# A fused two-layer kernel: when the steps of a second triangular inverse are issued, where a recurrence state is copied, and when a block of it is loaded

## The chip, the cores and the metric

The kernel runs on one core of a Trainium2 chip. Its time is the device time of one execution in microseconds, as the chip's profiler or the timed runs give it. The core has five instruction queues: TensorE (matmuls, PE in the profile, with the weight loads listed as PEld), VectorE (DVE), ScalarE (ACT), GpSimd (POOL) and SyncE (SP). Each takes its instructions in the order in which they were issued to it. Matmuls write to PSUM, which VectorE and ScalarE read.

## What is computed

Layer one is an RWKV-7 mixer over 256 tokens with 32 heads of 64, layer two an attention layer with compressed, selected and windowed keys; each is added to the residual, and a norm ends it. What matters here is the recurrence of the first layer:

```python
def wkv7_scan(r, w, k, v, a, b):
    ...
    def step(S, inp):
        r_t, w_t, k_t, v_t, a_t, b_t = inp
        sa = jnp.einsum('bhvk,bhk->bhv', S, a_t)
        S = S * w_t[:, :, None, :] + sa[..., None] * b_t[:, :, None, :] + v_t[..., None] * k_t[:, :, None, :]
        return S, jnp.einsum('bhvk,bhk->bhv', S, r_t)
    S0 = jnp.zeros((B, H, N, N), jnp.float32)
    _, o = lax.scan(step, S0, seq)
    return jnp.moveaxis(o, 0, 1)
```

After it each head's output is normalized, a bonus is added, it is multiplied by a gate, and it goes through the output projection w_o.

## The kernel before

Every large product is made of fp32 numbers split into a high and a low part, in three matmuls. ScalarE writes the high part of a weight tile (line 206, whi), VectorE the low part (line 191, wlo).

The recurrence is done in chunks: the 256 tokens are four chunks of 64. In a chunk the step-by-step recurrence becomes a triangular system of 64 by 64 for each head, whose inverse is needed. Two heads are an index x, and four heads (two of x by two of h) make a unit U; there are eight units. The inverse of a 64 by 64 triangle is put together from its two diagonal 32 by 32 triangles and a product of matrices. stage_t (line 799) computes all the 32 by 32 inverses on VectorE, for sixteen heads at a time, one triangle on each of the 128 partitions: stage_t(0) serves units 0 to 3 and ends before the scan, stage_t(1) serves units 4 to 7 and runs beside units 0 to 2 of it. It doubles the size of the inverted blocks four times, to 2, 4 (lines 834 to 848), 8 and 16 (dot, line 849: a multiplication on line 854, a sum on line 857, in up to two halves). Then it stores the inverse (tnd), ScalarE transposes it by four copies (line 882), and it is stored once more (yvd).

The scan loop (line 1261) goes over the units, and for each over twelve visits v: chunk c = v // 3 and part p = v % 3 of phase (line 1074).
- p = 0: TensorE removes the old state's part (line 1072, with the masked products AMA, "ama" in the trace) and adds that of the state (line 1088); ScalarE copies the result to X (line 1090).
- p = 1: TensorE multiplies X by the inverse Yb (line 1095); ScalarE copies to uv (line 1097).
- p = 2: TensorE makes the output (line 1101) and the state's increment pS (line 1104). VectorE makes the new state nxt: a copy for the first chunk (line 1107), an addition afterwards (line 1109). ScalarE scales it to the decayed state sP for the next chunk (line 1114). Then VectorE takes the output's statistics (line 1123, sta).

Between these parts the loop issues the work of the neighbours. NORM says in which visit the output of the unit before is normalized ("nmr", "v", "b", "g", "+", "z" on VectorE, pairs of digits on ScalarE, lines 1143 to 1157). AUX says in which visit the next unit is prepared: B0 and B1 (transposes, line 1041), G and Y (lines 1022 and 1031: the lower left block of the inverse, from Yb and A10), A0 and A1 (products, lines 1055 and 1057), M2, M0, M1 (masks on VectorE, line 1063: ama and amr), T (the finished unit's transposes, line 1164). scale_r (line 1005) makes VectorE's ar and mb (lines 1010 and 1011). load_y (line 908) loads Yb on GpSimd's queue in two parts of four transfers, q = 1 and q = 0; G needs the part q = 1. fill(n) puts n filler steps of the dense projections on TensorE (lines 626 to 628), as many as FILLL and FILL say for each visit; they keep TensorE at work while the small chain goes over the other engines.

The order of all five queues in this stage is the order of the program text: it is written by hand (manual_schedule, line 973). Only the inverse is placed by a planner, Sched (line 97). It holds a clock t in nanoseconds that fillers and phases move on. pump() goes once through the background generators: one that is due issues its instructions up to its next yield; a yielded number is the wait until it is due again, a yielded function is a condition that must hold first. In the scan stage_t(1) is the only one. Its waits are a cost estimate times PACE (line 821); at 0 each pump takes one step. The prologue of the scan (PROLOGUE, lines 1243 to 1258) pumps as often as its "V" step says; unit 0 does so nine times more at visit 2 (line 1281). load_a(4), in visit 8 of unit 2, requires that the second inverse has been issued (line 898), and pumps until it is.

```python
        for v in range(12):
            phase(U, v // 3, v % 3)
            ...
            sch.pump()
            if v == 11:
                finish(U, "rg")
```

finish(U, "rg") (line 1127) takes the statistics of a unit on VectorE, then a power on GpSimd (line 1136) and a copy "bon" out of PSUM on ScalarE (line 1137).

Of the kernel before, what the change touches and what calls it, by code (L numbers as in the profile page):

```python
# [12 lines left out]
AF = mybir.ActivationFunctionType  # L13
# [56 lines left out]
KPO = 3  # L70
KLAG = 2
AUX = {2: ("B0",), 3: ("G",), 4: ("B1", "Y"), 7: ("A0",), 9: ("A1",), 10: ("T", "M2"), 11: ("M0", "M1")}
NORM = {1: ("nmr", "v", "02"), 2: ("b", "24"), 5: ("46",), 6: ("68",), 7: ("g",), 8: ("+", "z")}
FILLL = (3, 4, 4, 0, 0, 5, 4, 0, 4, 0, 4, 4)
PROLOGUE = ("R0", "R1", 6, "G", "B0", 4, "I", "Y", "B1", 2, "A0", 2, "V10", "A1", "M2", "M0", "M1", 2)
ZHOOK = 9
PACES, PACE = (0.0, 1.8, 1.8, 1.8), [0.0]
FILL = (3, 4, 4, 0, 0, 5, 4, 0, 4, 0, 4, 4)
FILLO, LASTFILL = 4, 36
QZ = (0, 25, 24, 1, 2, 23, 22, 21, 3, 20, 19, 18, 4, 17, 16, 15, 14, 13, 12, 11, 10)  # L80
# [137 lines left out]
def hybrid_kernel(ctx: ExitStack, tc: tile.TileContext, a: dict, out: bass.AP):  # L218
    nc = tc.nc
    V, S, G, PE = nc.vector, nc.scalar, nc.gpsimd, nc.tensor  # L220
# [578 lines left out]
    def stage_t(b):  # L799
# [49 lines left out]
        def dot(out, aa, bb, ni, nj, kk):  # L849
            x = X[:, :ni * nj * kk].rearrange("p (i j k) -> p i j k", i=ni, j=nj)  # L850
            m = 2 if b and ni * nj * kk > 512 else 1
            for i0, i1 in [(ni * n // m, ni * (n + 1) // m) for n in range(m)]:
                sh = [128, i1 - i0, nj, kk]
                V.tensor_tensor(x[:, i0:i1], aa[:, i0:i1, None, :].to_broadcast(sh), bb[:, None, :, :].to_broadcast(sh), op=OP.mult)  # L854
                if b:
                    yield pace(1.1 * (i1 - i0) * nj * kk)
                V.tensor_reduce(out[:, i0:i1], x[:, i0:i1], axis=AX.X, op=OP.add)
                yield pace(1.2 * (i1 - i0) * nj * kk) if b else pace(2.3 * ni * nj * kk + 60.0)

# [31 lines left out]
    NU = NK // 2  # L891
# [182 lines left out]
    def phase(U, c, p):  # L1074
# [18 lines left out]
        elif p == 1:  # L1093
            for x, h in each:
                PE.matmul(pu[R[1 - h], 1 - x], Yb[U % 2][H(x, h), x, c, :], XS[U][H(x, h), x, :], start=False, **mm)
            for h in range(2):
                S.activation(uv[R[1 - h], :, c, h, :], pu[R[1 - h]], AF.Copy)
            sch.t += 200
        else:
            for x, h in each:  # L1100
                PE.matmul(O[H(x, h), x], AMR[U % 2][:, h, x, c, :], uv[:, 1 - x, c, h, :], start=False, **mm)
            if c < NCH - 1:
                for x, h in each:
                    PE.matmul(pS[R[h], x], BKT[U % 2][x][:, c, h, :], uv[:, 1 - x, c, h, :], start=False, **mm)
                nxt = scan.tile([128, 2, 64], F32, name="S", bufs=3)
                if c == 0:
                    V.tensor_copy(nxt, pS)
                else:
                    V.tensor_tensor(nxt, SST[U][1], pS, op=OP.add)
                dec = None  # L1110
                if c < NCH - 2:
                    dec = scan.tile([128, 2, 64], F32, name="sP", bufs=2)
                    for x in range(2):
                        S.activation(dec[:, x], nxt[:, x], AF.Copy, scale=PCH[U][:, x, c:c + 1])
                SST[U] = (nxt, dec)
            sch.t += 700

# [143 lines left out]
    for U in range(NU):  # L1261
        PBK[U] = pair_tile(U % 2)
        P = U - 1
        PACE[0] = PACES[min(U + 1, 3)]
        for v in range(12):
            phase(U, v // 3, v % 3)
            if v % 3 == 2:
                stats(U, v // 3)
            sch.pump()
            if v == 11:  # L1270
                finish(U, "rg")
                if U + 2 < NU:
                    load_y(U + 2, qs=(1,))
            if v == 0:
                if U and U + 1 < NU:
                    load_y(U + 1, qs=(0,))
# [32 lines left out]
    U = NU - 1  # L1309
# [520 lines left out]
```

## Time and profile before

| | us |
|---|---|
| median of three timed runs | 1134.08 |
| the three runs | 1135.6, 1134.08, 1131.72 |
| the profiled execution | 1132.65 |
| its span, first to last instruction | 1130.9 |
| scan loop, first matmul of unit 0 to the end of unit 7 | about 366 to 566 |

A profile line such as "365.98 0.40 PE L1072 MATMUL pair<-uv,ama ... x8 [1.65 <-DVE ama L1063]" reads: at 365.98 us, for 0.40 us, eight matmuls of line 1072 on TensorE that write a tile of name pair from uv and ama; TensorE had been idle for 1.65 us, and what ended that was VectorE's instruction of line 1063 that writes ama. A line of the waits gives the waiting engine, the line and the releaser, then the sum in us, the number of times and the longest. A line of the stretches gives the window and its length, then for PE, PEld, DVE, ACT and POOL the busy us and the number of instructions, then the granted TensorE clock (1.00 is full speed), the busy share of the DMA engines and GB/s. A line of the instruction groups gives the number of instructions, their busy us and the mean ns of one. A line on a source line's instructions gives their least, middle and longest ns, and the first and last start. "who waited for it" lines give us and times.

### The profile page before, as it was taken

How to read it: one execution, taken by the hardware profiler on the slowest of the kernel's cores; microseconds unless marked ns; L12 is line 12 of the kernel's file. 1: busy time of each engine (PE TensorE's matmuls, PEld its weight loads, DVE VectorE, ACT ScalarE, POOL GpSimd, SP SyncE). 2: the span in 40 equal slices, each digit the busy share in tenths (PEclk: the TensorE clock that was granted, in tenths of full speed). 3: DMA queues.
4: the chain of work that ended last, by engine and by line, in shares of the span. 5: the costliest groups of instructions: out<-in, count | busy, mean ns of one | idle time of the engine just before them, and what ended most of it. 6: DMA issues, size and time to landing. Idle time of an engine off the chain costs nothing.

```text
span 1130.9 us, 25651 instructions
## 1 busy us (share of the span) xinstructions
PE 1105.1 (98%) x9496; PEld 979.3 (87%) x9496; DVE 829.2 (73%) x1776; ACT 723.8 (64%) x1704; POOL 316.1 (28%) x412
## 2 busy tenths in 40 slices
PE   8999999999999998999999999999999999999997
PEld 7788899898988988898888888888989999999887
DVE  6999876689897887566667876764666877766564
ACT  7667877577764446565556766665656777766553
POOL 1300045424347446453000010100323332332012
PEclk9999999999999989999999999999999999999999
DMA  7558878877879868775578658585746365544862
GB/s 256 156 193 258 231 209 261 241 215 219 258 216 285 211 170 217 205 191 147 159 233 272 211 175 286 179 276 165 195 145 165 100 155 140 136 131 149 299 196 103
DMA packets 234462, 226.33 MB, mean 200 GB/s; under 512 B 50608, under 2 KB 184096, under 8 KB 233952
## 3 DMA queue, kind: packets, MB, share of 16 engines
q1 hardware_dynamic: 228976, 219.14, 65.5%
q0 software_dynamic: 4896, 4.95, 1.9%
q8 instruction: 75, 1.23, 0.5%
q10 hardware_dynamic: 464, 0.59, 0.1%
q14 instruction: 51, 0.42, 0.1%
HBM read 200.48 MB, written 24.15 MB: 199 GB/s over the span
## 4 chain that ended last, share of the span: by engine, by line
PE 80%; DVE 9%; DMA 3%; issue 3%; ACT 3%; SPq 1%; POOL 1%; POOLq 0%; DVEq 0%; ACTq 0%
PE bank L609 13%; PE bank L611 13%; PE bank L608 13%; PE bank L626 7%; PE bank L628 7%; PE bank L627 7%; PE bank L234 5%; DVE wlo L191 3%; PE pair L611 1%; PE pair L608 1%; PE pair L609 1%; DMA Yb<-yvd 1%; PE bank L1181 1%; ACT whi L206 1%; DVE invX L854 1%
## 5 line engine op out<-in xcount | busy, mean ns | idle before, releaser
L191 DVE TENSOR_TENSOR wlo<-wraw,whi 128x512 fp32r<-128x512 f32 (+2 forms) x616 | 438.7, 725 | 160.2 <-ACT whi L206 156.3
L206 ACT ACTIVATE whi<-wraw 128x512 fp32r<-128x512 f32 (+2 forms) x664 | 403.4, 618 | 188.2 <-PE bank L611 69.3
L626 PE MATMUL bank<-mh,whi 128*128 128x256 f32 (+1 forms) x800 | 236.5, 296 | 0.4 <-ACT whi L206 0.4
L628 PE MATMUL bank<-mh,wlo 128*128 128x256 f32 (+1 forms) x800 | 229.6, 287 | 0.4 <-issue 0.4
L627 PE MATMUL bank<-ml,whi 128*128 128x256 f32 (+1 forms) x800 | 229.2, 286 | 0.0
L609 PE MATMUL bank<-wlo,mh 128*128 128x512 f32 (+3 forms) x576 | 218.0, 379 | 0.8 <-DVE wlo L191 0.7
L611 PE MATMUL bank<-whi,ml 128*128 128x512 f32 (+3 forms) x576 | 215.3, 376 | 0.0
L608 PE MATMUL bank<-whi,mh 128*128 128x512 f32 (+3 forms) x576 | 190.3, 377 | 0.6 <-ACT Vt L1474 0.3
L626 PEld LDWEIGHTS bank<-mh,whi 128*128 128x128 f32 (+1 forms) x800 | 153.0, 191 | 5.9 <-ACT whi L206 1.0
L628 PEld LDWEIGHTS bank<-mh,wlo 128*128 128x128 f32 (+1 forms) x800 | 153.0, 191 | 2.1 <-issue 0.6
L627 PEld LDWEIGHTS bank<-ml,whi 128*128 128x128 f32 (+1 forms) x800 | 153.4, 192 | 1.5
L609 PEld LDWEIGHTS bank<-wlo,mh 128*128 128x128 f32 x576 | 108.3, 188 | 17.9 <-DVE wlo L191 1.8
L611 PEld LDWEIGHTS bank<-whi,ml 128*128 128x128 f32 x576 | 108.3, 188 | 16.2
L608 PEld LDWEIGHTS bank<-whi,mh 128*128 128x128 f32 x576 | 107.0, 188 | 17.1 <-ACT Vt L1474 0.7
L191 POOL TENSOR_TENSOR wlo<-wraw,whi 128x512 fp32r<-128x512 f32 (+2 forms) x48 | 57.5, 1198 | 186.1 <-ACT whi L206 162.9
L609 PE MATMUL bank<-wlo,kvh 128*128 128x512 f32 x192 | 76.0, 396 | 0.0
L611 PE MATMUL bank<-whi,kvl 128*128 128x512 f32 x192 | 75.2, 392 | 0.0
L608 PE MATMUL bank<-whi,kvh 128*128 128x512 f32 x192 | 66.5, 391 | 0.0
L422 ACT ACTIVATE mh<-mtmp 128x256 fp32r<-128x256 f32 x95 | 37.7, 410 | 17.7 <-DVE mtmp L429 16.6
L429 DVE SCALAR_TENSOR_TENSOR mtmp<-xx,prm,xn 128x256 f32<-128x256 f32 x95 | 46.7, 503 | 0.1
L609 PEld LDWEIGHTS bank<-wlo,kvh 128*128 128x128 f32 x192 | 36.1, 188 | 7.8 <-issue 0.4
L423 DVE TENSOR_TENSOR ml<-mtmp,mh 128x256 fp32r<-128x256 f32 x95 | 40.2, 438 | 2.6 <-ACT mh L422 2.5
(350 smaller groups left out, 1908.9 us busy)
## 6 DMA issues: line engine op xcount, KB each, us to landing
wraw<-in_a_w_rkvz_dram SPq DMA_DIRECT2D x128, 512.0 KB, 5.2
wraw<-in_kv_w_dram SPq DMA_DIRECT2D x48, 512.0 KB, 4.6
wraw<-in_b_w_in_dram SPq DMA_DIRECT2D x40, 512.0 KB, 4.2
wraw<-in_a_w_o_dram SPq DMA_DIRECT2D x32, 512.0 KB, 4.6
wraw<-in_b_w_o_dram SPq DMA_DIRECT2D x32, 512.0 KB, 3.8
spd<-sp SPq DMA_DIRECT2D x16, 642.0 KB, 5.5
spl<-spd SPq DMA_DIRECT2D x16, 642.0 KB, 6.5
wraw<-in_b_w_in_dram SPq DMA_DIRECT2D x24, 384.0 KB, 3.2
```

Source lines behind the costliest of these rows:

```text
L191: eng.tensor_tensor(lv, src, hv.bitcast(F32), op=OP.subtract)
L206: self.nc.scalar.activation(hv, src, AF.Copy)
L234: return fn(*args, **kw)
L422: S.activation(h, src, AF.Copy)
L423: V.tensor_tensor(l, src, h.bitcast(F32), op=OP.subtract)
L429: V.scalar_tensor_tensor(m, xx[:, k, :], mu[:, k:k + 1], xn[:, k, 1:], op0=OP.mult, op1=OP.add)
L608: PE.matmul(o, mh[:, ts], wh[:, 0, :], start=k == ends[0], stop=False)
L609: PE.matmul(o, mh[:, ts], wl[:, 0, :], start=False, stop=False)
L611: PE.matmul(o, ml[:, ts], wh[:, 0, :], start=False, stop=k == ends[1])
L626: PE.matmul(o, wh[:, s, :], mh, start=k == 0 and first, stop=False, **kw)
L627: PE.matmul(o, wh[:, s, :], ml, start=False, stop=False, **kw)
L628: PE.matmul(o, wl[:, s, :], mh, start=False, stop=k == NK - 1, **kw)
```

## The change

Four edits, all in the scan stage.
1. The inverse's multiplications and sums (lines 854 and 857) are not issued in visits 0, 1, 2 and 11 of units 1 to 7: a flag HOLD is set there, and the generator yields a condition that it be cleared. To make up for it PACE is 0.9 instead of 1.8 from unit 1 on. The prologue pumps five times ("V5") instead of ten ("V10").
2. The normalization's step "b" (line 1147) moves from visit 2 to visit 4.
3. The first chunk's state is copied out of PSUM by ScalarE instead of VectorE, and ScalarE makes the decayed state of that chunk straight from PSUM instead of from the copy.
4. The part q = 1 of Yb for the unit after the next is loaded in visit 10, instead of visit 11 behind finish(U, "rg").

```diff
-NORM = {1: ("nmr", "v", "02"), 2: ("b", "24"), 5: ("46",), 6: ("68",), 7: ("g",), 8: ("+", "z")}
+NORM = {1: ("nmr", "v", "02"), 2: ("24",), 4: ("b",), 5: ("46",), 6: ("68",), 7: ("g",), 8: ("+", "z")}
...
-PROLOGUE = ("R0", "R1", 6, "G", "B0", 4, "I", "Y", "B1", 2, "A0", 2, "V10", "A1", "M2", "M0", "M1", 2)
+PROLOGUE = ("R0", "R1", 6, "G", "B0", 4, "I", "Y", "B1", 2, "A0", 2, "V5", "A1", "M2", "M0", "M1", 2)
...
-PACES, PACE = (0.0, 1.8, 1.8, 1.8), [0.0]
+PACES, PACE, HOLD = (0.0, 1.8, 0.9, 0.9), [0.0], [False]
...
                 sh = [128, i1 - i0, nj, kk]
+                if HOLD[0]:
+                    yield lambda: not HOLD[0]
                 V.tensor_tensor(x[:, i0:i1], aa[:, i0:i1, None, :].to_broadcast(sh), bb[:, None, :, :].to_broadcast(sh), op=OP.mult)
                 if b:
                     yield pace(1.1 * (i1 - i0) * nj * kk)
+                if HOLD[0]:
+                    yield lambda: not HOLD[0]
                 V.tensor_reduce(out[:, i0:i1], x[:, i0:i1], axis=AX.X, op=OP.add)
...
                 if c == 0:
-                    V.tensor_copy(nxt, pS)
+                    S.activation(nxt, pS, AF.Copy)
                 else:
                     V.tensor_tensor(nxt, SST[U][1], pS, op=OP.add)
...
-                        S.activation(dec[:, x], nxt[:, x], AF.Copy, scale=PCH[U][:, x, c:c + 1])
+                        S.activation(dec[:, x], (nxt if c else pS)[:, x], AF.Copy, scale=PCH[U][:, x, c:c + 1])
...
         for v in range(12):
+            HOLD[0] = U > 0 and v in (0, 1, 2, 11)
             phase(U, v // 3, v % 3)
             if v % 3 == 2:
                 stats(U, v // 3)
             sch.pump()
+            if v == 10 and U + 2 < NU:
+                load_y(U + 2, qs=(1,))
             if v == 11:
                 finish(U, "rg")
-                if U + 2 < NU:
-                    load_y(U + 2, qs=(1,))
```

## The prediction

> **What bounds the kernel now.** I read the page first, then the waits between 365 and 545 us (the stage in which the diff acts), then the same stage stretch by stretch, and last the order of single instructions on VectorE, GpSimd and TensorE.
>
> ```profile
> span 1130.9 us, 25651 instructions
> PE 1105.1 (98%) x9496; PEld 979.3 (87%) x9496; DVE 829.2 (73%) x1776; ACT 723.8 (64%) x1704; POOL 316.1 (28%) x412
> ...
> PE 80%; DVE 9%; DMA 3%; issue 3%; ACT 3%; SPq 1%; POOL 1%; POOLq 0%; DVEq 0%; ACTq 0%
> ```
>
> TensorE is busy 98% of the span and makes 80% of the chain that ended last. So a microsecond that TensorE stands still, or runs at half clock, is a microsecond of the end; work on another engine costs nothing until TensorE waits for it. In the scan stage it waits for these:
>
> ```profile
> PE pair L1022 <- DMA Yb<-yvd: 2.2, 6, 0.9
> PE pair L1072 <- DVE sta L1123: 2.1, 2, 1.2
> PE pair L1095 <- ACT X L1090: 1.7, 2, 0.9
> PE pair L1072 <- DVE ama L1063: 1.6, 1, 1.6
> PE bank L1041 <- DVE mb L1011: 1.3, 1, 1.3
> ```
>
> These five kinds of wait are 8.9 us. The stage loses more than that, because a wait also delays what hangs behind it and because the clock falls (the figure after the five engines' busy times, the granted clock):
>
> ```profile
> 365.00:390.00 25.00, 24.02 (x456) 22.00 (x456) 20.54 (x67) 10.02 (x29) 9.68 (x18) 0.86 0.93 239
> 390.00:415.00 25.00, 23.08 (x472) 20.91 (x471) 20.48 (x47) 12.52 (x38) 12.83 (x21) 0.86 0.68 170
> ...
> 451.02:469.48 18.46, 17.42 (x401) 15.65 (x400) 10.11 (x23) 10.32 (x31) 7.86 (x15) 1.00 0.75 198
> ```
>
> In the first two rows the clock is 0.86 and VectorE is busy 20.5 of 25 us; in the third it is 1.00 and VectorE has 10.1 of 18.5. The difference on VectorE is the second inverse, which is spread over units 0 to 2. To get the whole loss I compare equal stretches: every unit does the same twelve visits, and the first matmuls of visits 0, 3, 6 and 9 (line 1072) mark them.
>
> ```profile
> 365.98 0.40 PE L1072 MATMUL pair<-uv,ama 64*64 64x64 f32 x8 [1.65 <-DVE ama L1063]
> ...
> 375.24 0.34 PE L1072 MATMUL pair<-uv,ama 64*64 64x64 f32 x8
> ...
> 390.92 0.34 PE L1072 MATMUL pair<-uv,ama 64*64 64x64 f32 x8
> ...
> 407.26 0.34 PE L1072 MATMUL pair<-uv,ama 64*64 64x64 f32 x8
> ...
> 418.47 0.34 PE L1072 MATMUL pair<-uv,ama 64*64 64x64 f32 x8
> ...
> 440.16 0.34 PE L1072 MATMUL pair<-uv,ama 64*64 64x64 f32 x8
> ...
> 452.19 0.34 PE L1072 MATMUL pair<-uv,ama 64*64 64x64 f32 x8
> ...
> 458.17 0.34 PE L1072 MATMUL pair<-uv,ama 64*64 64x64 f32 x8
> ...
> 476.42 0.34 PE L1072 MATMUL pair<-uv,ama 64*64 64x64 f32 x8
> ...
> 483.16 0.34 PE L1072 MATMUL pair<-uv,ama 64*64 64x64 f32 x8
> ...
> 494.66 0.34 PE L1072 MATMUL pair<-uv,ama 64*64 64x64 f32 x8
> ...
> 501.04 0.34 PE L1072 MATMUL pair<-uv,ama 64*64 64x64 f32 x8
> ...
> 506.02 0.34 PE L1072 MATMUL pair<-uv,ama 64*64 64x64 f32 x8
> ...
> 511.59 0.34 PE L1072 MATMUL pair<-uv,ama 64*64 64x64 f32 x8
> ...
> 524.74 0.34 PE L1072 MATMUL pair<-uv,ama 64*64 64x64 f32 x8
> ...
> 530.63 0.34 PE L1072 MATMUL pair<-uv,ama 64*64 64x64 f32 x8
> ```
>
> Unit 5 is the clean one. Its visits 0-2 take 501.04 - 494.66 = 6.38 us, visits 3-5 take 506.02 - 501.04 = 4.98, visits 6-8 take 511.59 - 506.02 = 5.57. Against it:
> - before unit 0: the wait of 1.65 us for the masked products ama;
> - unit 0, visits 0-2: 375.24 - 365.98 = 9.26, which is 2.88 too long with no wait in it: the first stretch at half clock;
> - unit 1, visits 0-5: 407.26 - 390.92 = 16.34 against 11.36, 4.98 too long: waits for sta and X, and the second stretch at half clock (the like of the first, about 2.9);
> - unit 2, visits 0-8: 440.16 - 418.47 = 21.69 against 16.93, 4.76 too long: waits for mb, sta, X and the transposed inverse's copies on ScalarE;
> - visits 3-5 of units 3, 4 and 6, where Yb arrives late: 5.98, 6.74 and 5.89 against 4.98, 3.67 too long in all.
>
> The sum is 1.65 + 2.88 + 4.98 + 4.76 + 3.67 = 17.94 us. This is all that the change can take away.
>
> **The prologue, "V10" to "V5".** Ten pumped steps of the inverse stand on VectorE ahead of ama, for which TensorE waits. In the trace nine instructions start from the first row below up to the second; five pumped steps fewer are just these nine.
>
> ```profile
> 363.15 0.22 DVE L837 TENSOR_TENSOR invX<-invA,invT 128x64 f32<-128x64 f32 x1
> ...
> 365.24 0.68 DVE L1063 TENSOR_TENSOR ama<-bank,cst 128x512 f32<-128x512 f32 x1
> ```
>
> So ama moves up by 365.24 - 363.15 = 2.09 us, more than the wait of 1.65; its products come ahead of the last filler matmuls, so nothing else holds it. The wait goes to 0, and TensorE itself is late next. The nine instructions move into visits 0 and 1 of unit 0, where VectorE waited for TensorE; they cost nothing there unless B0 (line 1041) or sta become late, by at most their own 2.09 us. I take 0.
>
> **The inverse out of visits 11, 0, 1 and 2, at twice the pace.** I worked the scheduler's clock through both versions. Now the long steps (128x512 and 128x384) lie also in visits 11 to 2 of units 1 and 2, ahead of the mask, of mb, of the state copy and of sta. Afterwards none does, except one multiplication in visit 11 of unit 0, which is not held. Seventeen steps then fall into visits 3 to 10 of unit 1 (seven of 128x512, six of 128x384, four of 128x256), and the last six into visits 3 to 5 of unit 2. The inverse is still placed before load_a(4) in visit 8 of unit 2, which asks for it; only the four copies on ScalarE (line 882) and the store slip from visits 4-6 to visits 7-8. Their mean times:
>
> ```profile
> L857 DVE TENSOR_REDUCE invM<-invX 128x32 f32<-128x512 f32 x2 | 1.4, 683 | 0.0
> ...
> L854 DVE TENSOR_TENSOR invX<-invA,invM 128x384 f32<-128x384 f32 x2 | 1.7, 872 | 0.0
> ...
> L857 DVE TENSOR_REDUCE invM<-invX 128x32 f32<-128x384 f32 x2 | 1.1, 542 | 0.0
> ...
> L857 DVE TENSOR_REDUCE invM<-invX 128x64 f32<-128x256 f32 x1 | 0.4, 422 | 0.0
> ```
>
> Seventeen steps are 7 x 0.683 + 6 x 0.542 + 4 x 0.422 = 9.7 us. The like stretch of unit 3, from sta of visit 2 to sta of visit 11, is the row 451.02:469.48: 10.1 us of VectorE in 18.5 us, and 17.5 without unit 3's 1.0 us for Yb. So VectorE needs 9.7 + 10.1 = 19.8 us where TensorE needs 17.5. Where TensorE itself still loses the 0.7 us that I leave it in that stretch (below), it is 1.6; so VectorE comes out of unit 1 between 1.6 and 2.3 us late, and the first matmuls of unit 2 wait that long for sta of visit 11. I take 1.9, the middle. That is a new wait which this trace does not have. Of the other waits 0.7 is left at visits 3-4 of unit 1 (half of the two there, since vt and wlo still stand before sta), and 0.9 in unit 2, where the six last steps and ScalarE's four copies lie. "b" at visit 4 takes one 128x512 step out of the way of the state; it is in the sum of unit 1, since that row holds it.
>
> **State on ScalarE.**
>
> ```profile
> L1107 DVE COPY S<-pair x8: 275/291/292, 373.5 to 546.9; 128x128 f32<-128x128 f32 x8
> ...
> L1114 ACT ACTIVATE sP<-S,pc x32: 332/340/351, 373.9 to 553.7; 128x64 f32<-128x64 f32 x32
> ...
>   ACT bon L1137: 14.6, 8
> ...
> 499.53 0.35 DVE L1123 BATCH_NORM_STATS2 sta<-pair 128x6 f32<-128x64 f32 x2
> ```
>
> Eight copies of 0.29 us leave VectorE, where each stood behind vt and wlo, and the two scalings wait for TensorE alone. ScalarE gets eight copies; no row shows one, so I bound it by the first two rows, 0.29 and 0.34 us, and hide it behind the filler matmuls of visit 2. The change adds a wait. The third row (of those who waited for sta, line 1123) shows that a read of a unit's PSUM tile on ScalarE, bon, waits for VectorE's read of the same tile, 8 times of 8. So sta of visit 2 will wait for the copy and both scalings, 0.29 + 2 x 0.34 = 0.97 us; behind it on VectorE stands a wlo, and line 1072 of visit 3 waits for sta. In unit 5 sta ended at 499.88, 1.16 us ahead of that matmul at 501.04: so 0 in units 3 to 7, and 0.97 each, 7.8 in all, if that cover were gone. A scaling out of PSUM instead of SBUF I bound by -0.05 and +0.05 us, the difference of those two rows, and take 0.
>
> **The half clock.** Both stretches (2.88 and about 2.9 us) begin at waits, of 1.65 us for ama and of 1.2 for sta with one for X (under 0.9) close behind. I take them for their consequence, and gone with them. [...]
>
> **Yb one visit earlier.**
>
> ```profile
> 470.56 1.66 POOL L1136 TENSOR_TENSOR rg<-rg,half 128x8 f32<-128x8 f32 x1 [6.55 <-DVE rg L1135]
> 472.18 1.15 POOL L914 DMA_DIRECT2D Yb<-yvd  x2
> ```
>
> The first part of Yb is issued on GpSimd's queue behind rg, which waited 6.55 us for VectorE. Issued in visit 10 it is past both, needs only that visit's line 1095 and load_a's eight issues before it, and leads by rg's 1.66 us at least, against waits of at most 0.9. All 3.67 go. Rg can be held back by four issues of about 0.57, less than its 6.55. In unit 2 the inverse's store slips, but load_a asks for it first.
>
> **The sum.** 17.94 less 1.9, 0.7 and 0.9 is 14.4 us. The profiled execution took 1132.65 us (its span of 1130.9 and 1.75 around it), so its like takes 1118.2. The three timed runs have a mean of 1133.8, 1.1 above the profiled one: I forecast 1119.3. No edit of the stage after the scan is made; I cost it at nothing.
>
> **Rivals.**
>
> *Half clock behind the new wait.* A wait of 1.65 and the pair for sta and X were each followed by half clock; the 1.3 for mb was not. The new wait of 1.9 at the start of unit 2 lies above that. If it brings one stretch, 2.9 comes back: 1122.2. Against it: the visits around it are filled with large matmuls.
>
> *The half clock has another cause.* If the two stretches don't come from the waits, they stay, 2.88 + 2.9: 1125.1. For it: nothing but their order in time ties them. Against it: unit 3, with waits of under 1 us, runs at 1.00 (third row of the stretches). [...]
>
> *VectorE is later than I think.* The row of 0.872 us for 128x384 shows what a step can take beside GpSimd, 0.33 more than the other. If all seventeen take that, 5.6 us more come on top of the 1.9: 1124.9, and 1127.8 with a half-clock stretch.
>
> *The waits only move.* VectorE does the same work but for eight copies. If units 0 to 2 lose as much in other places, only Yb's part is won, 3.67 at most: 1130.1 to 1134.
>
> *Slower: the state on ScalarE in every unit.*
>
> ```profile
> L206 ACT ACTIVATE whi<-wraw 128x512 fp32r<-128x512 f32 (+2 forms) x664 | 403.4, 618 | 188.2 <-PE bank L611 69.3
> ```
>
> There the copy stands behind two scalings like sP and a whi of 0.62, 1.30 us. With the 0.97 of the copy and its scalings sta is 2.27 us later than the state's matmuls allow; 1.16 is covered. Seven units would lose 1.1 each, 7.8, which still leaves it faster. From a gap of about 1.65 us, where half clock set in, each would lose 2.9 more: 7 x (1.1 + 2.9) = 28 us, thus 1147.3. For it: ScalarE's queue is fixed by hand. Against it: it waits for VectorE now, and would start sooner.
>
> **How the numbers follow.** Forecast 0.46, half clock behind the new wait 0.20, another cause 0.10, VectorE later 0.10, moved waits 0.08, slower 0.06. A measurement of this kernel tells 0.3%, 3.4 us, from no change. So faster has 0.86, same 0.08, slower 0.06. The forecast's own range is 1117.4 (a new wait of 1.6 and nothing else left) to 1121 (2.3, and 0.2 a unit for sta); the timed runs scatter by 2 us below their mean, so 1115 is the low end; the high end of 1127 takes in the half clock, its other cause and VectorE's lateness up to near its end. That leaves out 0.18.
>
> **What would show it.** Right: no wait for ama before unit 0; clock 1.00 in both stretches; 6.4 us for visits 0-2 of units 1 and 2; no wait of line 1022 for Yb; sta waiting for sP on VectorE; a wait of 1 to 2.3 us for sta at the first matmul of unit 2. Wrong: a VectorE without idle time through all of unit 1 and waits over 3 us behind it; clock below 1 in the scan; line 1072 waiting for sta in visit 3 of units 3 to 7.

## The result and the profile after

The changed kernel took 1128.18 us, the median of five runs (1126.91 to 1129.11), beside 1133.96 for the kernel before: a ratio of 0.9938, 95% interval 0.9921 to 0.9956. That is 5.8 us less, where the forecast said 14.4, and above the top of its range (1127). Six later runs of the same kernel had a median of 1125.89 beside 1134.68 (0.9919, 0.9894 to 0.9944), 8.8 us less: inside the range, but still far from 14.4. The direction was right; the size was not.

The page of the changed kernel, with the span, the engines' busy times and the chain that ended last:

```profile
span 1126.6 us, 25651 instructions
PE 1100.2 (98%) x9496; PEld 973.9 (86%) x9496; DVE 830.0 (74%) x1768; ACT 723.0 (64%) x1712; POOL 316.1 (28%) x412
...
PE 79%; DVE 10%; DMA 4%; issue 3%; ACT 3%; POOL 1%; SPq 0%; POOLq 0%; DVEq 0%; ACTq 0%
```

Eight instructions went from VectorE to ScalarE; nothing else changed in kind. TensorE's waits between 365 and 545 us in it:

```profile
PE pair L1076 <- DVE sta L1127: 2.9, 5, 1.0
PE bank L626 <- ACT whi L206: 1.6, 1, 1.6
PE pair L1092 <- issue: 1.3, 1, 1.3
PE pair L1059 <- issue: 1.1, 1, 1.1
PE pair L1099 <- ACT X L1094: 0.7, 1, 0.7
```

(In the changed kernel the lines from 854 on stand two, and those from 857 on four further down: 1022 is 1026, 1072 is 1076, 1088 is 1092, 1095 is 1099, 1123 is 1127.) The waits for ama, mb and Yb are gone. sta has more than before (2.9 for 2.1), and so have the waits named "issue", in which TensorE waited for nothing that the profile shows; the kernel before has 2.3 us of them in the scan with its prologue. The clock in the two stretches that were at 0.86:

```profile
365.00:390.00 25.00, 24.01 (x513) 21.64 (x513) 21.89 (x78) 10.55 (x30) 13.28 (x24) 1.00 1.10 280
390.00:415.00 25.00, 23.66 (x501) 21.51 (x500) 23.56 (x54) 13.81 (x41) 13.50 (x24) 1.00 0.78 194
```

It is 1.00 in this execution. VectorE, in the third busy figure, is busy 23.6 of 25 us in unit 1. The marks (first matmul of a group of three visits) of units 2 and 5:

```profile
415.47 0.34 PE L1076 MATMUL pair<-uv,ama 64*64 64x64 f32 x8
424.24 0.34 PE L1076 MATMUL pair<-uv,ama 64*64 64x64 f32 x8 [0.71 <-DVE sta L1127]
429.37 0.34 PE L1076 MATMUL pair<-uv,ama 64*64 64x64 f32 x8
436.51 0.34 PE L1076 MATMUL pair<-uv,ama 64*64 64x64 f32 x8
...
489.99 0.34 PE L1076 MATMUL pair<-uv,ama 64*64 64x64 f32 x8
496.50 0.34 PE L1076 MATMUL pair<-uv,ama 64*64 64x64 f32 x8
501.62 0.34 PE L1076 MATMUL pair<-uv,ama 64*64 64x64 f32 x8
```

Unit 2 still takes 436.51 - 415.47 = 21.04 us for visits 0-8 (21.69 before). Unit 5, which nothing was to touch, is longer: 6.51 for 6.38 in visits 0-2, 5.12 for 4.98 in visits 3-5.

One profile is a small sample of a kernel whose runs scatter by 2 us, so I took two of the kernel before and three of the changed one. The table adds their stretches, each a difference of two marks, from the first matmul of line 1022 in the scan's prologue to visit 9 of unit 7.

| stretch | before (us) | after (us) | change of the means | forecast |
|---|---|---|---|---|
| prologue to unit 0 | 10.82, 10.97 | 9.98, 8.76, 8.27 | -1.9 | -1.65 |
| unit 0, visits 0-2 | 9.26, 7.81 | 7.23, 7.45, 7.49 | -1.15 | -2.88 |
| unit 0, visits 3-11 | 15.68, 16.10 | 16.33, 17.08, 16.52 | +0.75 | 0 |
| unit 1, visits 0-5 | 16.34, 13.57 | 12.52, 13.64, 13.37 | -1.8 | -4.28 |
| unit 1, visits 6-11 | 11.21, 11.22 | 11.89, 11.21, 11.22 | +0.2 | +1.9 |
| unit 2, visits 0-8 | 21.69, 23.42 | 21.04, 22.57, 20.39 | -1.2 | -3.86 |
| units 3, 4, 6, visits 3-5 | 18.61, 18.38 | 15.37, 15.35, 17.99 | -2.3 | -3.67 |
| units 3 to 6, visits 0-2 | 25.50, 25.50 | 26.46, 26.96, 27.56 | +1.5 | 0 |
| unit 3, visits 6-8 | 6.23, 6.44 | 7.26, 7.11, 5.87 | +0.4 | 0 |
| the rest | | | -0.2 | 0 |
| all | 206.10, 204.25 | 198.90, 200.51, 199.34 | -5.6 | -14.4 |

(The forecast's new wait of 1.9 us stands ahead of the first matmul of unit 2, so it falls into the last visits of unit 1.) The sum agrees with the timed 5.8. No row is worse than forecast by more than 2.7 us: the shortfall is spread.

### The profile page after: what moved, and what is told of

Read it like the earlier page. It is cut to its first block, busy times and chain, and to the rows that moved or that the text cites. A ratio compares the mean times of both kernels' runs of the same rounds, so it can differ in the third digit from the quotient of the medians.

```text
span 1126.6 us, 25651 instructions
## 1 busy us (share of the span) xinstructions
PE 1100.2 (98%) x9496; PEld 973.9 (86%) x9496; DVE 830.0 (74%) x1768; ACT 723.0 (64%) x1712; POOL 316.1 (28%) x412
## 4 chain that ended last, share of the span: by engine, by line
PE 79%; DVE 10%; DMA 4%; issue 3%; ACT 3%; POOL 1%; SPq 0%; POOLq 0%; DVEq 0%; ACTq 0%
PE bank L609 13%; PE bank L611 13%; PE bank L608 13%; PE bank L626 7%; PE bank L628 6%; PE bank L627 6%; PE bank L234 5%; DVE wlo L191 4%; ACT whi L206 1%; PE pair L611 1%; PE pair L608 1%; PE pair L609 1%; DVE invX L856 1%; PE bank L1185 1%; DMA vt<-vd 1%
```

## The experiments

The theory after the first look at the trace was that every edit wins what it aims at, but that the copy on ScalarE, the loads ahead of rg and VectorE's lateness give part of it back. The rivals: the waits only move; the half clock has another cause; the loss is chance. All medians below come with the kernel before on the same chip (1133.87, 1134.85, 1133.94, 1134.25 and 1134.68 us in the five groups).

### The edits one by one

Yb alone, on the kernel before:

```diff
+            if v == 10 and U + 2 < NU:
+                load_y(U + 2, qs=(1,))
             if v == 11:
                 finish(U, "rg")
-                if U + 2 < NU:
-                    load_y(U + 2, qs=(1,))
```

> The kernel before with only the Yb loads moved (two DMAs of the q = 1 half issued ahead of rg). Theory A (the gains of the three edits exist one by one, and the trace of the changed kernel shows them: Yb -3.2, half clock and the wait for ama -6.6, the state copy on ScalarE +0.26 a unit, the rest new waits): 3.2 us faster than before, line 1022 no longer waits for Yb in visits 3 to 5 of units 3, 4 and 6, rg on GpSimd runs about 2 us later behind the DMA issues without a TensorE wait from it, since the copy of the state does not stand behind O on ScalarE here. Rival B (waits only move): under 1 us faster, with a wait for sta at line 1072 in place of the one for Yb.

Measured 1129.91 us, ratio 0.997 (0.9958 to 0.9983), 4.0 less; no wait for Yb was left. But a wait of 0.34 to 0.41 us for X at line 1095 took the place of part of it: visits 3 to 5 of units 3 to 6 take 5.37 to 5.42, not 4.98.

The inverse's edits alone (V5, pace, HOLD, "b"):

```diff
-PACES, PACE = (0.0, 1.8, 1.8, 1.8), [0.0]
+PACES, PACE, HOLD = (0.0, 1.8, 0.9, 0.9), [0.0], [False]
...
+            HOLD[0] = U > 0 and v in (0, 1, 2, 11)
```

> The kernel before with only the edits of the inverse's steps (V5, pace, held visits, the b step to visit 4). Theory A: granted clock 1.00 in units 0 and 1 (two stretches of about 2.9 us back) and no wait for ama ahead of unit 0, less about 1 us of VectorE's lateness at the start of unit 2: 4.5 to 6 us faster than before. Rival B (the half clock has another cause than the gaps of the first units): a granted clock below 1 stays in units 0 and 1, and the gain is under 1.5 us. [...]

Measured 1129.46, ratio 0.9967 (0.9953 to 0.9981), 4.4 less. No wait for ama was left, and visits 0-2 of unit 1 took 6.38 as forecast; but visits 0-2 of unit 2 took 7.99, and a stretch at half clock stood in its visits 3 to 5. Two stretches around it:

```profile
413.00:424.00 11.00, 8.41 (x164) 7.32 (x164) 10.67 (x27) 5.38 (x16) 7.15 (x11) 0.99 0.63 145
424.00:431.00 7.00, 7.00 (x95) 6.15 (x91) 3.36 (x8) 3.97 (x11) 0.39 (x1) 0.52 0.70 220
```

TensorE was busy 8.41 of 11 us, and for the next 7 the clock was 0.52. This is near the place of the prediction's first rival, but not that rival: no wait for sta stands there, and the last waits ahead of the stretch are 1.07 and 0.20 us for Yb, at 422.60 and 423.08, which the early load takes away.

The state on ScalarE alone:

```diff
-                    V.tensor_copy(nxt, pS)
+                    S.activation(nxt, pS, AF.Copy)
...
-                        S.activation(dec[:, x], nxt[:, x], AF.Copy, scale=PCH[U][:, x, c:c + 1])
+                        S.activation(dec[:, x], (nxt if c else pS)[:, x], AF.Copy, scale=PCH[U][:, x, c:c + 1])
```

> The kernel before with only the copy of the first chunk's state on ScalarE and sP straight from PSUM. Theory A: the chain by which the first matmul of visit 3 waits is longer by 0.26 us in each unit, and more where the copy stands behind O on ScalarE: 2 to 3 us slower than before, visits 0 to 2 of unit 5 up from 6.38 to 6.5. Rival B (the prediction: nobody waits for the copy, as the chain through sP and sta sets the time): within 1 us of before, visits 0 to 2 of unit 5 at 6.38.

Measured 1133.31, ratio 0.9991 (0.9975 to 1.0006): no difference that can be told. Visits 0 to 2 of units 3 to 6 stay at 6.37 and 6.38, as the prediction had it. So theory A missed here: by itself the copy costs the chain nothing in these units.

The changed kernel without the state's edit:

> The changed kernel with the copy of the state back on VectorE, and sP made from the copy. Theory A: the 0.26 us of each unit come back (2.1), and the waits for sta in visit 3 of units 2 and 3, where the copy stood behind O in ScalarE's queue, shrink by another 1: 2 to 3 us faster than the changed kernel, 1125 to 1126. Rival B: VectorE, which is nearly full in unit 1, is later still with the copy, and the time is the changed kernel's or up to 1 us more.

Measured 1127.13, ratio 0.9942 (0.9925 to 0.9958): the changed kernel's time, where theory A had 1125 to 1126. Visits 0-2 of unit 1 fell from 7.41 to 6.62 us and those of units 4 to 6 to 6.37 and 6.38, but visits 3-5 rose to 5.37 and more. In these two pairs (with and without it, on the kernel before and on the changed one) the state's edit is worth nothing that can be told. In the second it only shifts where a delay on ScalarE shows.

### Where that delay comes from

The same instruction in unit 4 of the kernel before, and then of the changed kernel, both on VectorE:

```profile
473.36 0.15 DVE L1143 SCALAR_TENSOR_TENSOR nmr<-mv,rg 128x8 f32<-128x8 f32 x1
```

```profile
470.45 0.76 DVE L1147 SCALAR_TENSOR_TENSOR nmr<-mv,rg 128x8 f32<-128x8 f32 x1
```

In units 4 to 6 nmr takes 0.15 to 0.16 us in each kernel that loads the part q = 1 of Yb in visit 11, and 0.76 to 0.77 in each that loads it in visit 10, and O on ScalarE waits for it. What follows stands in ScalarE's queue; here is the run without the state's edit, on ScalarE and then on TensorE:

```profile
469.90 0.68 ACT L1161 ACTIVATE O<-pair,nmr,rg 128x64 f32<-128x64 f32 x2
470.48 0.48 ACT L1046 ACTIVATE bkt<-bank 128x384 f32<-128x384 f32 x1
470.85 0.63 ACT L206 ACTIVATE whi<-wraw 128x512 fp32r<-128x512 f32 x1
471.37 0.27 ACT L1094 ACTIVATE X<-pair 128x128 f32<-128x128 f32 x1
...
471.70 0.34 PE L1099 MATMUL pair<-X,Yb 64*64 64x64 f32 x8 [0.36 <-ACT X L1094]
```

ScalarE runs without a pause from O to X, and TensorE waits 0.36 us for X. With the state on ScalarE the same lateness hits the copy and, through sP and sta, the first matmul of visit 3. Unit 2 of the changed kernel shows it at its worst, ScalarE and then VectorE:

```profile
421.90 0.70 ACT L1161 ACTIVATE O<-pair,nmr,rg 128x64 f32<-128x64 f32 x2 [2.67 <-DVE nmr L1147]
422.50 0.63 ACT L206 ACTIVATE whi<-wraw 128x512 fp32r<-128x512 f32 x1
423.02 0.27 ACT L1111 ACTIVATE S<-pair 128x128 f32<-128x128 f32 x1
423.18 0.53 ACT L1118 ACTIVATE sP<-pair,pc 128x64 f32<-128x64 f32 x2
...
423.74 0.36 DVE L1127 BATCH_NORM_STATS2 sta<-pair 128x6 f32<-128x64 f32 x2 [0.72 <-ACT sP L1118]
```

O waits 2.67 us for nmr, the copy waits behind O and whi, sta waits 0.72 for sP, and the matmul at 424.24 (above) waits 0.71 for sta. The edit took the copy off VectorE and put it behind VectorE.

I first took nmr's 0.6 us for the four q = 0 loads that GpSimd issues beside it, and moved those to visit 2, once with the state on VectorE and once as in the change:

```diff
-                if U and U + 1 < NU:
-                    load_y(U + 1, qs=(0,))
...
+            if v == 2 and U and U + 1 < NU:
+                load_y(U + 1, qs=(0,))
```

> The changed kernel with the copy of the state on VectorE (as in the run without the state's edit, 1127.1) and the four Yb loads of the q = 0 half issued on GpSimd in visit 2, behind nmr and pc and ars, instead of in visit 0. Theory A (nmr takes 0.76 us instead of 0.16 where GpSimd issues those four loads beside it, ScalarE's O and with it the X of visit 3 start that much later, and TensorE waits at line 1099): nmr back at 0.16 in units 2 to 6, the waits for X at line 1099 (3.5 us in 6 places) down by 1.5 to 2 us, 1125 to 1125.6. Rival B (the 0.76 us have another cause): nmr stays at 0.76, and the time is within 1 us of 1127.1.

> The changed kernel, the copy of the state on ScalarE as there, with the four Yb loads of the q = 0 half issued in visit 2 as in the run beside this one. Theory A: nmr at 0.16 us, O on ScalarE 0.6 us earlier, and the copy of the state, which is queued behind O, with it: visits 0 to 2 of units 4 to 6 from 6.50 to 6.38, visits 3 to 5 from 5.12 to 4.98, and 0.3 to 0.5 off the wait for sta in units 2 and 3: 1.3 to 2 us under the changed kernel, 1126.2 to 1126.9. Rival B: the 0.13 us each come from ScalarE's longer way to sP, not from nmr, and stay: 1128.

Measured 1124.53 (0.991, 0.9895 to 0.9925) and 1129.4 (0.995, 0.9929 to 0.997). nmr stayed at 0.76 in both, although the first time was even lower than theory A had it. This does not clear GpSimd, because another of its instructions had moved into the loads' place, here in unit 4 of the first of the two runs:

```profile
467.10 0.84 POOL L1017 TENSOR_TENSOR ars<-spl 128x384 f32<-128x384 f32 x1 [0.43 <-DVE spl L1014]
```

```profile
467.20 0.76 DVE L1147 SCALAR_TENSOR_TENSOR nmr<-mv,rg 128x8 f32<-128x8 f32 x1
```

In units 4 to 6 of every run with the late q = 0 loads nmr starts 0.1 us behind ars and ends 0.02 to 0.03 behind it. With q = 1 loaded early and q = 0 left in visit 0 it lies beside q = 0 loads and takes as long; in units 5 and 6 of the kernel before it lies beside a q = 1 load and takes 0.15 to 0.16. The first of the two runs, repeated:

> The run with the state's copy on VectorE and the late q = 0 loads once more, beside the other two on the same chip. Theory A: 1124.5 within 1.5 us, issue waits in the scan 1 to 3 us in all. Rival B (its lead of 3.6 us on the changed kernel was chance): 1126 to 1129.

gave 1126.74 (0.9937, 0.9911 to 0.9962). Why nmr is longer stays open. The kernels of 1124.53 and 1129.4 differ by the state's edit alone: the one with the state on VectorE was 4.9 us faster, clear of the scatter, and 2.7 in the repeat, which is not clear of it. So with the late loads the edit does seem to cost something, unlike in the two pairs above. That ScalarE's order carries its cost to TensorE was tried by moving O's second pair behind the X of visit 3, with the state on VectorE and the late q = 0 loads:

```diff
-NORM = {1: ("nmr", "v", "02"), 2: ("24",), 4: ("b",), 5: ("46",), 6: ("68",), 7: ("g",), 8: ("+", "z")}
+NORM = {1: ("nmr", "v", "02"), 4: ("24", "b"), 5: ("46",), 6: ("68",), 7: ("g",), 8: ("+", "z")}
```

> The run with the state's copy on VectorE and the late q = 0 loads, with the second pair of O's rows (step 24) on ScalarE moved from visit 2 to visit 4. Theory A (with Yb early nmr takes 0.76 us, O comes 0.6 us later on ScalarE, and the X of visit 3 stands behind O's second pair): X comes 0.68 us sooner, the waits for X at line 1099 (4.3 us in 7 places) fall under 1.5, visits 3 to 5 of units 4 to 6 from 5.4 to 4.98: 2 to 3 us faster, about 1122. Rival B (ScalarE is late in visit 4 instead, and uv or Yb are waited for): within 1 us of 1124.5.

```profile
487.46 0.34 PE L1076 MATMUL pair<-uv,ama 64*64 64x64 f32 x8
...
493.84 0.34 PE L1076 MATMUL pair<-uv,ama 64*64 64x64 f32 x8
...
498.82 0.34 PE L1076 MATMUL pair<-uv,ama 64*64 64x64 f32 x8
```

Unit 5 is clean again: 6.38 and 4.98. Measured 1125.41 (0.9918, 0.9896 to 0.9941). So with the state on VectorE the order on ScalarE is the whole of the loss in visits 0 to 5 of units 4 to 6. The time that theory A gave, about 1122, did not come. Once more, beside the changed kernel:

> The version with the state's copy on VectorE, the late q = 0 loads and O's second pair in visit 4, once more. Theory A: 1124 to 1126 and 2 to 3 us under the changed kernel beside it, visits 3 to 5 of units 4 to 6 at 4.98. Rival B (its lead was chance): within 1 us of the changed kernel.

> The changed kernel once more, beside the best version on the same chip. Theory A (what holds it back is fixed by its program): 1127 to 1129, issue waits of TensorE in the scan over 4 us, 1.2 us or more of them in visits 6 to 8 of units 2 and 3 each, visits 3 to 5 of units 4 to 6 at 5.12. Rival B (its first five runs were a draw of chance): under 1126, issue waits under 3 us.

Measured 1125.07 (0.9911, 0.9885 to 0.9937) and 1125.89 (0.9919). The repaired version beats the kernel before clearly. Its lead of 0.8 us on the changed kernel is within the scatter, so by the times rival B stands in both; by the marks theory A does in part (4.98 and 5.12 us for visits 3 to 5 of units 4 to 6, and 4.1 us of issue waits in the changed kernel, but only 1.0 of them in visits 6 to 8 of unit 2 and none in unit 3).

### VectorE's lateness, and GpSimd behind it

The second inverse's dot products left out, and the hold widened over two more visits with the q = 0 loads late:

```diff
-            HOLD[0] = U > 0 and v in (0, 1, 2, 11)
+            HOLD[0] = U > 0 and v in (0, 1, 2, 9, 10, 11)
```

> The changed kernel without the dot products of the second inverse (its two outer levels, 8 and 16, are left out for units 4 to 7, so that the lower corners of their inverses are not computed): what those steps on VectorE still cost in the changed kernel at all. Theory A (VectorE's lateness at the end of unit 1 is a loss that the hold only moved): visits 0 to 2 of units 1 and 2 near 6.5 each (from 7.4 and 8.8), no half clock in units 1 and 2 in any run, 3 to 5 us faster than the changed kernel, 1123 to 1125. [...]

> The changed kernel with the q = 0 loads in visit 2 and the hold on the inverse's steps widened from visits 0, 1, 2, 11 to 0, 1, 2, 9, 10, 11: about 2.3 us of products and sums leave visits 9 and 10 of unit 1 for visits 6 to 8 of unit 2. Theory A: VectorE is no longer late at the start of unit 2, visits 0 to 2 of unit 2 fall from 8.8 to under 7.2, and the half clock that sits behind that wait in some runs is gone: 1.5 to 2.5 us under the run with the late loads alone, about 1124.5. Rival B (the steps only make VectorE late in visits 6 to 8 of unit 2 instead): what visits 0 to 2 gain, visits 6 to 8 of unit 2 lose, and the two runs agree within 1 us.

Without the products: 1128.13 (0.9939, 0.9923 to 0.9954), no gain. Units 2 and 3 begin in 6.5 us as theory A has it, but the inverse's last transfers now come in unit 0, hold rg on GpSimd, and TensorE waits 2.6 us for sta in unit 1, where an issue wait of 3.4 us with a stretch at half clock behind it follows. With the wider hold: 1134.11 (0.9998, 0.9984 to 1.0011), all lost. Its marks in unit 2, and then a wait in unit 3:

```profile
415.87 0.34 PE L1076 MATMUL pair<-uv,ama 64*64 64x64 f32 x8
...
422.23 0.34 PE L1076 MATMUL pair<-uv,ama 64*64 64x64 f32 x8
...
427.21 0.34 PE L1076 MATMUL pair<-uv,ama 64*64 64x64 f32 x8
...
455.44 0.49 PE L1076 MATMUL pair<-uv,ama 64*64 64x64 f32 x8 [8.39 <-DVE sta L1127]
```

Visits 0-2 of unit 2 fall from 8.77 to 6.36 and visits 3-5 to 4.98: VectorE's lateness out of unit 1 is worth 2.4 us there. But steps that are moved out of unit 1 end later, and the price is paid in unit 3. GpSimd shows why:

```profile
442.90 0.56 POOL L918 DMA_DIRECT2D Yb<-yvd  x1
444.73 1.09 POOL L918 DMA_DIRECT2D Yb<-yvd  x2 [1.27 <-DMA a<-abd]
...
450.38 1.68 POOL L1140 TENSOR_TENSOR rg<-rg,half 128x8 f32<-128x8 f32 x1
```

rg stands behind load_a, which waits for the second inverse, and behind Yb. (2.63 us of the delay, ahead of another transfer at 449.33, are idle time of GpSimd that the profile puts down to nothing.) So GpSimd holds nmr, which starts at 452.08 after VectorE has waited 8.05 us for rg; VectorE's next sta starts at 454.93, and TensorE waits 8.39 us for it. The changed kernel has the same chain, only shorter:

```profile
442.60 2.18 POOL L918 DMA_DIRECT2D Yb<-yvd  x4
444.80 1.68 POOL L1140 TENSOR_TENSOR rg<-rg,half 128x8 f32<-128x8 f32 x1
```

Between the loads and rg GpSimd has no pause; in its three profiles the first matmul of visit 3 in unit 3 waits 0.51, 1.0 and 1.6 us for sta. A milder spread (pace 1.4, 0.9, 0.4, held visits 0, 1, 2, 10, 11, state on VectorE, late q = 0 loads):

> The run with the state's copy on VectorE and the q = 0 loads in visit 2 (1124.5), with the inverse's steps spread otherwise: pace factors 1.4 (unit 0), 0.9 (unit 1) and 0.4 (unit 2) in place of 1.8, 0.9 and 0.9, held visits 0, 1, 2, 10, 11. Theory A (what is left at the starts of units 2 and 3 is VectorE's lateness at the end of unit 1, and GpSimd's, which issues the second inverse's last transfers ahead of rg of unit 2): the last product in visit 5 of unit 2 as before, visit 10 of unit 1 without steps; visits 0 to 2 of unit 2 from 8.1 to under 7, of unit 3 from 7.7 to under 7.2, 1.5 to 2.5 us faster, about 1122.5. Rival B (unit 0's VectorE has no room for what is moved there): waits for X, sta or mb in unit 0 and at the start of unit 1 take it back, 1124 to 1126.

Measured 1126.34 (0.9931, 0.9905 to 0.9956). Visits 0-2 of unit 2 took 6.37, better than theory A, and of unit 3 6.99; no gain in time, since unit 1 took 0.9 longer in visits 0-2 and a half clock stretch came in unit 3.

### The waits for nothing

The second profiles:

> The kernel before, a second profile. Theory A (a stretch of half clock follows each 3.41 us window in which TensorE idles over about 1.6 us, and where the windows fall is chance): one to three such stretches, granted clock 0.990 to 0.995, at the wait ahead of unit 0 or in the first visits of units 1 and 2, the same waits by line as in the first profile, but TensorE's waits that nothing in the profile explains ('issue') between 1 and 6 us in the scan and at the same lines as there within some us of place; the scan's first instruction anywhere within 1.5 us of 355.2. Rival B (all is fixed by the program): the half clock at 366 and 400, 2.3 us of issue waits, the scan's start at 355.2 within 0.3.

> The changed kernel, a second profile. Theory A: the waits for sta at line 1076 are the first profile's (2.9 us in 5 places) within 0.5 us, since the program fixes them, while the issue waits (6.1 us there) are anywhere from 1.5 to 6 and the scan's start (357.5 there) is within 1.5 us of 355.9; a half clock stretch behind the start of unit 2 may be there or not. Rival B: issue waits of 6 us at the same five lines and a scan's start at 357.5, that is, they belong to the changed program and are part of the loss.

The 3.41 us and the 1.6 us of idle TensorE were read off the traces; the rows of the first profile stand with the half clock in the next section. The kernel before, 1132.54 us, had waits for sta, ama and X within 0.3 us of the first profile's, half clock again (behind ama and in unit 2), and issue waits of 2.3 us as in the first. The changed kernel, 1129.24, had sta waits of 2.5 and issue waits of 6.2 (6.1 in the first, 4.1 in the third profile). So these are not mere chance, and rival B was nearer. Over all profiles they are 4.1 to 7.3 us in the seven with the state on ScalarE, and 0.7 to 4.0 in the eleven with it on VectorE (means 5.7 and 2.5); the kernels differ in other things too. In unit 2 and unit 3, first the kernel before, then it with the state's edit alone:

```profile
434.38 0.45 PE L1088 MATMUL pair<-S,ars 64*64 64x64 f32 x13 [0.40 <-issue]
...
459.58 0.39 PE L628 MATMUL bank<-mh,wlo 128*128 128x256 f32 x1 [0.41 <-issue]
```

```profile
434.10 0.46 PE L1088 MATMUL pair<-S,ars 64*64 64x64 f32 x15 [1.61 <-issue]
...
461.14 0.39 PE L626 MATMUL bank<-mh,whi 128*128 128x256 f32 x1 [1.18 <-ACT O L1157]
```

The same places, four and three times as long. (The named O of the last line is no cause: line 626 doesn't read it. The 1.6 us at line 626 in the changed kernel, put down to a whi, are of this kind too: in the run with the state's edit alone the same matmul starts while that whi is still being written, so it reads the whi before, which in the changed kernel had ended 1.85 us earlier.) Of the 78 such waits in the 18 profiles 72 end 2.2 to 3.1 us after the start of a transfer on queue q8, one of two that the page calls instruction: 75 packets of 16 KB in all, each of which took 0.88 to 1.60 us in the first profile of the kernel before, where four such waits end 2.42 to 2.84 us after the start of one. That the transfers make the waits is not shown. The other six stand at the line of Y in the prologue (1031, 1035 in the changed kernel), among them the 1.6 us of the changed kernel's first profile. What the edit adds to TensorE's program is eight wait instructions at the first matmuls of visits, in the kernel before and in that with the edit:

```profile
L1072 PEldq EVENT_SEMAPHORE  x8: 51/576/615, 362.9 to 539.9; - x8
```

```profile
L1072 PEldq EVENT_SEMAPHORE  x16: 51/51/579, 362.5 to 550.9; - x16
```

Whether the place of the instructions in TensorE's program or the copy itself makes the waits was tried with other added instructions, on the version with the state on VectorE; a wait of over 1 us in visits 6 to 8 of unit 2 or 3 would speak for the place, none over 0.7 for the copy:

```diff
-            for c in range(NCH - 1):
+            for c in (0, *range(NCH - 1)):
                 PE.transpose(bt[:, c * 128:c * 128 + 128], BK[:, c].rearrange("p x t -> p (x t)"), ident)
```

> The run with the state's copy on VectorE and the late q = 0 loads, with the first of the three transposes of each B step done twice (the same data to the same place, 16 more weight loads and 16 more matmuls in all, some 0.16 us each): it moves TensorE's later instructions by 2 to 4 places a unit, as the state's copy on ScalarE does with its 8 more wait instructions. [...]

```profile
386.69 0.58 PE L627 MATMUL bank<-ml,whi 128*128 128x256 f32 x1 [2.05 <-issue]
...
456.00 0.34 PE L1092 MATMUL pair<-S,ars 64*64 64x64 f32 x8 [1.06 <-issue]
```

Measured 1128.08 (0.9942, 0.9922 to 0.9961). A wait of 1.06 came in unit 3 and one of 2.05 in unit 0; neither profile of its base has one over 0.8. That speaks for the place of the instructions and against the copy as the cause. But it is one profile, and one program's waits vary: the repaired version has one of 1.34 us at line 628 in unit 3 in its first profile and none there in its second. So what sets their length is not shown.

## Why the prediction was wrong

**Prologue: right.** No wait for ama of 1.65 was left (0 to 0.9 us in the profiles with V5), and 1.9 us went, for 1.65 forecast.

**Half clock: the tie to the waits and the mean right, "gone with them" too strong.** The two stretches in the first profile of the kernel before, and ahead of each the 3.41 us before it:

```profile
362.72:366.13 3.41, 1.76 (x50) 1.49 (x46) 3.10 (x13) 0.00 (x0) 2.87 (x6) 1.00 1.06 348
366.13:372.96 6.83, 6.83 (x77) 6.25 (x75) 6.22 (x19) 1.86 (x5) 3.90 (x7) 0.50 1.20 258
...
396.85:400.27 3.42, 1.77 (x61) 1.45 (x59) 3.42 (x10) 2.02 (x7) 1.68 (x4) 1.00 1.24 241
400.27:407.09 6.82, 6.55 (x74) 5.92 (x74) 3.54 (x9) 4.08 (x13) 0.00 (x0) 0.50 0.87 263
```

TensorE was idle for 1.65 us (3.41 less 1.76, 3.42 less 1.77), and then the clock was 0.50 for 6.83 us. The stretches were no fixed places: they came in unit 0 and unit 2 in the second. The mean clock of 80 timed runs of the kernel before is 0.9919, of 12 of the changed one 0.9968, which is worth at most 0.0049 x 1131 = 5.5 us, for 5.8 forecast (2.88 and about 2.9). But stretches still come behind other waits. The changed kernel's third profile, around the wait of 1.6 us in unit 3:

```profile
445.00:449.00 4.00, 2.40 (x72) 2.15 (x71) 3.31 (x6) 3.75 (x12) 3.54 (x7) 1.00 0.92 222
449.00:456.00 7.00, 7.00 (x91) 6.20 (x90) 2.01 (x8) 3.67 (x11) 0.19 (x1) 0.51 0.83 251
```

All stretches lie on a grid of 3.41 us in each trace: in that of the kernel before, the clock changes at 366.13, 372.96, 400.27, 407.09 and 1127.30 us, which is 6.83, 27.31, 6.83 and 720.21 us apart, or 2, 8, 2 and 211 times 3.413. Of the spaces of that grid in the scan that were at full clock, in the 18 traces, all 12 with 1.6 us or more of idle TensorE were followed by half clock, 4 of some 46 with 1.0 to 1.6, and none with less. So about half a space without work was enough, in one piece ahead of 366.13 (the wait for ama) and in two ahead of 400.27 (1.16 for sta, and 0.49 of the 0.76 for X).

**Yb: the waits gone, the size partly luck, two prices missed.** 4.0 us by itself, 3.67 forecast, and the waits for Yb gone. But in the profile of that run visits 3 to 5 of units 3, 4 and 6 won 2.3 us (16.20 for 18.61 and 18.38), and unit 5 lost 0.4. Part of the rest can be the clock: 0.9938 in the mean of its 12 runs, 0.9921 in the 27 of the kernel before, worth at most 0.0017 x 1134 = 1.9 us. "Rg can be held back by four issues of about 0.57, less than its 6.55" held in units 3 to 6, but not in unit 2, where the slipped store had filled GpSimd and rg left 2.1 us late in the first profile; and that nmr takes 0.6 us longer in units 4 to 6 with the early loads was put at nothing, although the kernel before has one such nmr, 0.76 us at 424.48 in unit 2.

**State on ScalarE: the step that failed in the chain.** "0 in units 3 to 7" compared the copy's 0.97 us with a cover of 1.16 at sta, and "it waits for VectorE now, and would start sooner" took the copy to be free of VectorE. It was, in the run with that edit alone. In the changed kernel it stands in ScalarE's queue behind an O that waits for nmr: 0.13 us a unit in visits 0-2 of units 4 to 6, 0.5 to 1.6 in unit 3, 0.3 to 0.8 in units 1 and 2 against the run without it. This is why "units 3 to 6, visits 0-2" went up by 1.5. The run without it pays for the same lateness in visits 3 to 5 instead (5.95 us in unit 3, 5.37 to 5.42 in units 4 to 6, for 5.12). So what the prediction put at nothing is the delay that an O behind a late nmr hands down ScalarE's queue; the copy only decides where it comes out.

**The sum: a term was missing.** TensorE's issue waits stood in the trace of before with 2.3 us, and the prediction left them out without a reason. They rose by 3.2 us (the mean of 6.1, 6.2 and 4.1, less 2.3), a large item beside a shortfall of 8.6; in the profiles the most of them stand in units 0 and 1 and in visits 6 to 8 of units 2 and 3. What they are worth in time is not shown: the run without the state's edit had 1.3 us of them and the changed kernel's time, while in the pair with the late q = 0 loads 4.3 us of them went with 1129.4, and 2.1 and 1.5 with 1124.53 and 1126.74.

**The new wait at unit 2: the lateness right, the wait at another place.** VectorE comes out of unit 1 as late as forecast: sta of visit 11 starts 0.9 to 1.4 us behind the first matmul of unit 2 in the three profiles, and 0.9 ahead of that of the next unit in units 2 to 6, which makes 1.8 to 2.3 us, for 1.6 to 2.3. (In the kernel before it was 0.9 late already. The row of 0.872 us in the rival "VectorE is later than I think" is the mean of 1.20 us, at 395.75 beside GpSimd's loads, and 0.55, at 399.00 with GpSimd idle. But steps of 128x512 took 0.69 and 0.68 us beside GpSimd's work, at 422.02 and 426.37, and 0.69 without, at 386.77; that GpSimd made the difference is not shown.) But "the first matmuls of unit 2 wait that long for sta of visit 11" failed: in none of the three does that matmul wait. The lateness reaches TensorE a little later, by other paths:

```profile
416.83 0.35 DVE L1127 BATCH_NORM_STATS2 sta<-pair 128x6 f32<-128x64 f32 x2
```

```profile
417.27 0.18 ACT L1141 ACTIVATE bon<-pair 128x8 f32<-128x8 f32 x1 [4.12 <-DVE sta L1127]
```

```profile
418.19 0.34 PE L1099 MATMUL pair<-X,Yb 64*64 64x64 f32 x8 [0.70 <-ACT X L1094]
...
419.92 0.39 PE L628 MATMUL bank<-mh,wlo 128*128 128x256 f32 x1 [0.60 <-DVE wlo L191]
```

On ScalarE X stands behind bon, which waits for sta (0.70 us on TensorE); wlo comes late from VectorE (0.60); and nmr, O and the copy delay sta of visit 3 (0.71, above). Visits 0-2 of unit 2 are 2.0 to 2.4 us longer than those of unit 5 before, and the run with the wider hold wins 2.4 there. So the 1.9 us were nearly right, by a mechanism that was not.

Since the parts overlap (half clock followed all 12 spaces with 1.6 us or more of idle TensorE), I don't add them up to the last microsecond. The repaired version, free of the losses in units 4 to 6, is still about 6 us above the forecast; what is left there is at the starts of units 2 and 3 and in unit 0.

## What to carry to other kernels

Moving a step to an idle engine moves it into that engine's queue: ask what stands ahead of it there and whom that waits for, before pricing its length (here an O behind a late nmr: 0.5 to 1.6 us in unit 3). When work on a shared planner slips, follow its last transfers to the queue on which they are issued, for what stands behind them can inherit the lateness (here rg, and TensorE's 8.39 us in the run with the wider hold). A loss that one profile shows (a stretch at half clock above all) should be priced by its mean over several, and a change can be worth less than the sum of its waits when others take their place (here 5.8 and 8.8 us, for 14.4).

## What was not expected of the hardware

TensorE waited 0.2 to 3.4 us in the middle of ready work, and 72 of the 78 such waits ended 2.2 to 3.1 us behind the start of a 16 KB transfer on q8, a queue that the page calls instruction; at one place in unit 2 the wait was 0.40 us in the kernel before and 1.61 with eight more wait instructions. Spaces of 3.41 us of the clock's grid with 1.65 us of idle TensorE were followed by two spaces, 6.83 us, at a clock of 0.50, both times in the first profile of the kernel before. After the standstill of 8.39 us in the run with the wider hold the clock was 0.98, 0.50 and 0.84 in the three stretches of 10 us from 440 on: 13.6 us at half clock, four spaces. And a VectorE instruction of 128x8 elements, nmr, took 0.15 to 0.16 us in units 4 to 6 with the part q = 1 of Yb loaded in visit 11, and 0.76 to 0.77 with it loaded in visit 10, by a cause that the runs did not settle: when the neighbouring loads were moved, ars stood beside it instead.
